# A two-layer trunk on one core: the last feed-forward output, with both column halves of a token tile in a row

## The chip, the cores and the metric

The kernel runs on one core of a Trainium2 chip. The metric is the device time of one execution in microseconds (us), as the median of several runs. The engines of the core are TensorE (PE; its weight loads are shown as PEld), VectorE (DVE), ScalarE (ACT) and GpSimd (POOL); SyncE (SP) issues most DMA transfers.

## What is computed

One inference step of a trunk of two layers, for 512 latent tokens and 128 prompt tokens of width 1024, in float32. Each layer does this (`ctx` are cached keys, values and states, which the latent tokens read; the mixers are differential attention, a gated delta network and HGRN2):

```python
def trunk_layer(x, mod, w_in, w_out, ..., ln_g, ln_b, w_ffn_in, w_ffn_out, ctx):
    shift_m, scale_m, gate_m, shift_f, scale_f, gate_f = jnp.split(mod, 6, axis=-1)
    z = (x * (1 + scale_m) + shift_m) @ w_in
    o, k_c, v_c, s_d, s_h = token_mixers(z, ..., ctx)
    x = layer_norm(ALPHA * x + gate_m * (o @ w_out), ln_g[0], ln_b[0])
    gt, up = jnp.split((x * (1 + scale_f) + shift_f) @ w_ffn_in, 2, axis=-1)
    x = layer_norm(ALPHA * x + gate_f * ((jax.nn.silu(gt) * up) @ w_ffn_out), ln_g[1], ln_b[1])
    return x, k_c, v_c, s_d, s_h
```

The feed-forward's hidden width is 2816. The outputs are x of both token groups, and keys, values and states of the prompt.

## The kernel before

**Tiling.** The 640 tokens are five tiles of 128 (tau 0 to 3 latent, 4 prompt; `NT` is 5). Products run in split float32: each operand is a high part and a low rest, and a product is three passes over them. A weight block is loaded by SP into `raw` (L256), cast to its high part `hl` by ScalarE (L275), and VectorE forms the rest; that is `unit`. `mm` (L175) is every matmul and `tt` (L178) every two-operand elementwise operation, whichever engine it is given, so these two lines hold much of the trace.

**Stages of a layer.** The input projections (names pa, pb, pc), the mixers (attention with the scores `pas`, HGRN with the products `ph` and its transposes `pth`; the modulation vectors of what follows, `psm`, run among them), the output projection `pop` with residual and normalisation, whose transposes are `pta`, and the feed-forward. In the mixers HGRN's queries `hq` (L588) and values `hv` (L589) and the attention's operands `aqs`, `aks`, `ack`, `avf` (L1154 to L1187) come from device memory, all by SP's queue.

**The feed-forward's output.** Its 22 blocks of 128 hidden columns go in six parts (`FF_PARTS`); the last holds four blocks, 18 to 21. A part's product is added into the residual `r` of each token tile, in two column halves of 512 (`nh`), so there are ten groups (nh, tau) of 12 matmuls each for the last part. Each group goes into a bank of PSUM `pfo`; VectorE multiplies it by the gate (`ft`, two buffers), GpSimd adds it to `r` (VectorE for tile 4), and VectorE takes the half's statistics (L1724). When half 1 of a tile is done, the tile can be normalised. In layer 0 that is `ln_next`: statistics joined, GpSimd takes the power -0.5, then for tiles 0 to 2 ScalarE normalises, VectorE scales and GpSimd shifts; for tiles 3 and 4 two VectorE operations do it (L545, L546). The result `xmf` is transposed by TensorE (`ptf`, L503) and split into `xT` by ScalarE (L505) and VectorE; from there layer 1's projections start, first `pbg`. In layer 1 it is `ln_last`: for tiles 0 to 2 the halves are shared between ScalarE with GpSimd and VectorE, for tiles 3 and 4 VectorE does all (L576, L577), and SP writes the output.

**What sets the order.** The order of the groups is the list `order` (L1700). A group is issued no sooner than the end of the group four before it (`OPEN`). The instructions of the whole kernel are then put in order for each engine by a scheduler that plays them on a timeline of its own; the code's order is its input, and its choices run on through what follows.

Of the kernel before, what the change touches and what calls it, by code (L numbers as in the profile page):

```python
# [25 lines left out]
NT = NTOK // P  # L26
# [85 lines left out]
def tile_trunk(  # L112
# [30 lines left out]
    def psum_phase(**classes):  # L143

        PS.clear()
        for names, tags in classes.items():
            cyc = {"tags": tags, "i": 0}
            for n in names.split("_"):
                PS[n] = cyc
# [15 lines left out]
    def psS(cls, name):  # L165
        ps = ps_next(cls, [P, 512], name)
        return ps[:, 0, :] if len(ps.shape) == 3 else ps
# [9 lines left out]
    def tt(eng, out, a, b, op):  # L177
        return eng.tensor_tensor(out, a, b, op)  # L178
# [22 lines left out]
    def pool(name, side):  # L201
        cm_ = tc.tile_pool(name=name, bufs=1, side=side, reuse_waits="tile")
        return cm_, cm_.__enter__()

    def close(cm_):
        cm_.__exit__(None, None, None)
# [90 lines left out]
    def gemm_N(ps, n, aT, tau, units, first=True, last=True):  # L297

        tot = sum(len(ks) for _, ks in units)
        j = 0  # L300
        for u, ks in units:
            for i, k in enumerate(ks):
                for q, (wi, xi) in enumerate(PASSES):
                    end = mm(ps[:, :n], (aT(xi, k) if callable(aT) else aT[:, xi, k])[:, tau * P:(tau + 1) * P], u[:, wi, i, :],
                       start=(first and j == 0 and q == 0), stop=(last and j == tot - 1 and q == 2))
                j += 1
        return end
# [4 lines left out]
    def rowunit(w, k0, nk, c0, n):  # L312
        return unit(w[k0 * P:(k0 + nk) * P, c0:c0 + n].rearrange("(k p) n -> p k n", p=P), nk, n)

    def bg_units(l):
        return [(rowunit(w_in[l], k0, nk, C_BG, NB), list(range(k0, k0 + nk))) for k0, nk in ((0, 3), (3, 3), (6, 2))]
# [171 lines left out]
    def rowload(pool, src, tag, t=None):  # L488
        if t is None:
            t = pool.tile([P, D], F32, tag=tag, bufs=1, name=tag)  # L490
        S.dma_start(t, src.partition_broadcast(P))
        return t

    def modvec(l, i, j):
        return modrow[l][j, i * D:(i + 1) * D]
# [13 lines left out]
    def affine(l, si, mi, ln, pool, tag, bufs):  # L509


        raw = pool.tile([P, 1024], F32, tag=tag, bufs=bufs, name="aff")
        v = raw[:32, :256].rearrange("p (k n) -> p k n", k=4)
        rows = [modrow[l][:, i * D:(i + 1) * D].rearrange("j (q n) -> j q n", n=64) for i in (si, mi)]
        for j in range(2):
            for k, src in enumerate((rows[0][j], rows[1][j], ln_g[ln], ln_b[ln])):
                S.dma_start(v[16 * j:16 * j + 16, k], src if k < 2 else src.rearrange("(q n) -> q n", n=64))
        V.tensor_scalar_add(v[:, 0], v[:, 0], 1.0)
        tt(V, v[:, 3], v[:, 0], v[:, 3], ALU.mult)
        tt(V, v[:, 1], v[:, 1], v[:, 3], ALU.add)  # L520
        tt(V, v[:, 0], v[:, 0], v[:, 2], ALU.mult)
        for j in range(2):
            for k in range(2):
                S.dma_start(rows[k][j], v[16 * j:16 * j + 16, k])

    def affine_rows(pool, l, si, mi, pre=None):

        return [[rowload(pool, modvec(l, i, j), f"{nm}{j}", pre and pre[2 * j + k])
                 for k, (i, nm) in enumerate(((si, "sc"), (mi, "sh")))] for j in range(2)]
# [20 lines left out]
    def ln_tile(r, mv, rs, g, b, tau):  # L550
        V.scalar_tensor_tensor(r[tau], r[tau], mv[:, tau, 0:1], g, ALU.subtract, ALU.mult)  # L551
        V.scalar_tensor_tensor(r[tau], r[tau], rs[:, tau, 0:1], b, ALU.mult, ALU.add)
# [795 lines left out]
    for l in range(DEPTH):  # L1348
# [258 lines left out]
        def pair_a(f):  # L1607
            if f not in gts:
                gate_unit(f)
            gt_ = gts.pop(f)  # L1610
            a_ = psS("g", f"pfa{l}_{f}")
            prod(a_, gt_, 0, "11")
            if 2 <= f < AHEAD:
                s1, sg = xtra[:, (f - 2) * 960:(f - 2) * 960 + HT], xtra[:, (f - 2) * 960 + HT:(f - 1) * 960]
            else:
                s1 = fp.tile([P, HT], F32, tag="s1", bufs=2, name=f"s1_{l}_{f}")
                sg = fp.tile([P, NTOK], F32, tag="sg", bufs=2, name=f"sg{l}_{f}")
            A.copy(s1, a_[:, :HT])
            prod(a_, gt_, 4, "12", start=False)
            A.activation(sg[:, :HT], a_[:, :HT], AF.Silu)  # L1620
            part_a[f] = (s1, sg)
# [46 lines left out]
        for part, (f0, f1) in enumerate(FF_PARTS):  # L1668
            nk = f1 - f0
            last = part == len(FF_PARTS) - 1  # L1670
            for f in range(f0, f1):
                end = pair_b(f, f - f0)
                if AHEAD - 1 <= f < NFF - 1:
                    pair_a(f + 1)
                if part == 0:
                    with tc.issue_after(end.ins):
                        for tau in range(f, NT if f == f1 - 1 else f + 1):
                            ln_tile(r, mv, rs, lg, lb_, tau)
            if part == 0 and l + 1 < DEPTH:
                affine(l + 1, 1, 0, (l, 1), praw, "raw", 3)  # L1680
            if part == 0:
                gf = [rowload(None, modvec(l, 5, j), None, t_) for j, t_ in enumerate((lg, lb_))]
            if last:
                close(sc_)
                close(hx)
                lc, lp = pool(f"M{l}", "left")
                WB[0] = 3
                if l + 1 < DEPTH:
                    rows = affine_rows(lp, l + 1, 1, 0)
                else:  # L1690
                    HL["seq"], HL["i"] = [(phl, "hl", 4), (lp, "hl", 2)], 0
                    lg2, lb2 = (rowload(lp, x_[l, 1], n_) for x_, n_ in ((ln_g, "lg2"), (ln_b, "lb2")))
                    psum_phase(g_n=PP1 + PP2 + QQ + RR)

            def out_units(nh):
                return [(rowunit(Wo, f0 + k0, 2, nh * 512, 512), [k0, k0 + 1]) for k0 in range(0, nk, 2)]

            usn, ends = {}, []
            skew = 1 if last else NT
            order = [(nh, tau) for i in range(NT + skew) for nh, tau in ((0, i), (1, i - skew)) if 0 <= tau < NT]  # L1700
            if last and l + 1 < DEPTH:
                HL["seq"], HL["i"] = [(phl, "hl", 4)], 0
                usn[0] = out_units(0)
                HL["seq"], HL["i"] = [(fp, "hb", 1), (lp, "hl", 1)], 0
                usn[1] = out_units(1)
                HL["seq"], HL["i"] = [(phl, "hl", 4)], 0
                bgu = bg_units(l + 1)
            for nh, tau in order:
                us = usn[nh] if nh in usn else usn.setdefault(nh, out_units(nh))
                cs = slice(nh * 512, (nh + 1) * 512)  # L1710
                j = 0 if tau < LT else 1
                ps = psS("n", f"pfo{l}_{part}_{nh}_{tau}")
                with ExitStack() as es:
                    if last and len(ends) >= OPEN:
                        es.enter_context(tc.issue_after(ends[-OPEN].ins))
                    ends.append(gemm_N(ps, 512, h_, tau, us))
                tmp = fp.tile([P, 512], F32, tag="ft", bufs=2, name="ft")
                tt(V, tmp, ps, gf[j][:, cs], ALU.mult)
                if part == 0:
                    V.scalar_tensor_tensor(r[tau][:, cs], r[tau][:, cs], ALPHA, tmp, ALU.mult, ALU.add)  # L1720
                else:
                    tt(V if last and tau >= 4 else G, r[tau][:, cs], r[tau][:, cs], tmp, ALU.add)
                if last:
                    V.bn_stats(st[tau][:, nh, :], r[tau][:, cs])  # L1724
                    if nh == 1 and l + 1 < DEPTH:
                        ln_next(lp, r[tau], st[tau], mv, rs, rows[j], xT, tau, f"f{l}_{tau}")
                    elif nh == 1:
                        dst = y_sample[0, tau * P:(tau + 1) * P, :] if tau < LT else y_prompt[0]
                        ln_last(r[tau], st[tau], mv, rs, lg2, lb2, tau, dst)
# [47 lines left out]
```

## Time and profile before

| | |
|---|---|
| Median of 3 runs | 2084.02 us (2083.7 to 2092.38) |
| Profiled execution | 2080.84 us |
| Span of its trace | 2078.9 us |
| PE / DVE / POOL / ACT busy | 92% / 69% / 42% / 38% of the span |
| Mean granted TensorE clock | 0.956 of full |
| Layer 0's mixers (first pas to first pop) | 351.45 to 521.88 us |
| Layer 0's last feed-forward output and what follows it | 1027.77 to 1071 us |
| Layer 1's mixers | 1370.19 to 1542.56 us |
| Layer 1's output projection | 1542.56 to 1620.68 us |
| Last feed-forward output, to the last normalisation | 2039.49 to 2075.30 us |

The span is the time from the trace's first instruction to its last. A share of busy time is a mean over stages that have different limits, so each stage has to be read by itself. In a row of the timeline, the bracket is the time that the engine stood idle before it, with an arrow to what released it.

### The profile page before, as it was taken

What the parts mean: (1) busy time and instruction counts of PE and PEld (TensorE: products, weight loads), DVE (VectorE), ACT (ScalarE), POOL (GpSimd) and SP (SyncE); (2) the same over time, 40 slices, a digit from 0 to 9 for tenths busy, and PEclk for the clock granted to TensorE, in tenths of its full rate; (3) what the DMA queues carried; (4) which work ended last, traced back from release to release, by engine and by line L of the source; (5) the groups of instructions that cost most, each with busy time, mean ns of one, the idle gap of its engine ahead of it and who ended that gap; (6) DMA issues with size and microseconds to landing.
All of it is one profiled execution on the core that took longest, in us unless ns stands there. A gap on an engine that the chain in (4) does not pass through costs nothing. (4 is left out here: it accounts for less than half of the span.)

```text
span 2078.9 us, 37821 instructions
## 1 busy us (share of the span) xinstructions
PE 1905.8 (92%) x14914; PEld 1676.6 (81%) x14914; DVE 1444.5 (69%) x2515; ACT 791.4 (38%) x1563; POOL 880.2 (42%) x986
## 2 busy tenths in 40 slices
PE   7999997788978999999999989977899799999996
PEld 5988986566758899989989979765687779989895
DVE  5458525898488866667676783459867897667677
ACT  3542322566143334333336323236752434334331
POOL 0375235775142132435155924358642311532444
PEclk7999999899999999999999999989899899999998
DMA  8423215866353323222434341376434233223222
GB/s 284 131 79 121 93 57 140 217 200 205 137 179 90 115 82 92 72 82 73 142 96 130 108 131 57 102 169 214 143 148 147 83 110 91 72 82 93 80 72 81
DMA packets 243255, 249.36 MB, mean 120 GB/s; under 512 B 19354, under 2 KB 190342, under 8 KB 243078
## 3 DMA queue, kind: packets, MB, share of 16 engines
q1 hardware_dynamic: 240486, 245.11, 38.6%
q8 instruction: 118, 1.93, 0.4%
q10 hardware_dynamic: 2592, 1.84, 0.3%
q14 instruction: 59, 0.48, 0.1%
HBM read 218.72 MB, written 28.18 MB: 119 GB/s over the span
## 5 line engine op out<-in xcount | busy, mean ns | idle before, releaser
L178 DVE TENSOR_TENSOR hl<-raw,hl 128x1024 fp32r<-128x1024 f32 (+1 forms) x210 | 281.4, 1344 | 87.5 <-ACT hl L275 70.6
L175 PE MATMUL pfo<-hl,ha 128*128 128x512 f32 x1320 | 312.7, 395 | 1.6 <-ACT hl L275 1.1
L175 PEld LDWEIGHTS pfo<-hl,ha 128*128 128x128 f32 x1320 | 246.2, 187 | 60.5 <-DVE ha L178 1.4
L178 POOL TENSOR_TENSOR r<-r,ft 128x512 f32<-128x512 f32 x96 | 143.4, 1513 | 241.1 <-DVE ft L178 238.4
L178 POOL TENSOR_TENSOR t<-raw 128x512 f32<-128x512 f32 x44 | 66.2, 1504 | 337.0 <-DMA raw<-in_w_ffn_in_dram 168.2
L175 PE MATMUL pfc<-sx,hl 128*128 128x320 f32 x1056 | 173.8, 313 | 9.5 <-ACT hl L1553 7.2
L175 PE MATMUL pfa<-xT,hl 128*128 128x320 f32 x1056 | 173.2, 314 | 4.5 <-DVE hl L178 3.0
L275 ACT CAST hl<-raw 128x1024 fp32r<-128x1024 f32 (+2 forms) x122 | 125.8, 1036 | 132.9 <-DMA raw<-in_w_ffn_out_dram 49.7
L175 PEld LDWEIGHTS pfc<-sx,hl 128*128 128x128 f32 x1056 | 161.8, 190 | 12.9 <-ACT hl L1553 7.8
L1553 ACT CAST hl<-raw 128x1024 fp32r<-128x1024 f32 x88 | 92.0, 1051 | 203.8 <-PE pfo L175 105.4
L175 PEld LDWEIGHTS pfa<-xT,hl 128*128 128x128 f32 x1056 | 161.9, 192 | 7.3 <-DVE hl L178 3.8
L175 PE MATMUL paq<-xT,hl 128*128 128x320 f32 x768 | 123.9, 318 | 0.6 <-ACT az L1241 0.6
L175 PE MATMUL pop<-hl,xT 128*128 128x512 f32 x480 | 120.7, 403 | 0.0
L175 PEld LDWEIGHTS paq<-xT,hl 128*128 128x128 f32 x768 | 116.3, 191 | 3.5 <-issue 1.2
L175 PEld LDWEIGHTS pop<-hl,xT 128*128 128x128 f32 x480 | 88.4, 190 | 24.8 <-issue 6.6
L178 DVE TENSOR_TENSOR ft<-pfo,lg 128x512 f32<-128x512 f32 x96 | 63.9, 683 | 51.2 <-PE pfo L175 41.5
L178 DVE TENSOR_TENSOR t<-raw,t 128x512 f32<-128x512 f32 x88 | 73.9, 840 | 36.0 <-POOL t L178 35.8
L178 POOL TENSOR_TENSOR hK<-hK,hT 64x256 f32<-64x256 f32 x120 | 87.0, 725 | 27.1 <-PE ph L175 21.2
L175 PE MATMUL pfd<-xT,h 128*128 128x320 f32 x528 | 86.2, 313 | 9.6 <-DVE u L178 9.6
L175 PE MATMUL pbq<-xT,hl 128*128 128x320 f32 x576 | 89.5, 312 | 1.2 <-DVE hl L178 0.4
L175 PE MATMUL pfb<-sx,hl 128*128 128x320 f32 x528 | 89.2, 311 | 0.6 <-DVE hl L178 0.6
L175 PEld LDWEIGHTS pfd<-xT,h 128*128 128x128 f32 x528 | 80.0, 190 | 11.1 <-issue 8.5
(409 smaller groups left out, 4198.6 us busy)
## 6 DMA issues: line engine op xcount, KB each, us to landing
raw<-in_w_ffn_in_dram SPq DMA_DIRECT2D x96, 512.0 KB
raw<-in_w_mod_dram SPq DMA_DIRECT2D x80, 512.0 KB
raw<-in_w_in_dram SPq DMA_DIRECT2D x56, 512.0 KB
raw<-in_w_ffn_out_dram SPq DMA_DIRECT2D x44, 512.0 KB
pc<-in_w_mod_dram SPq DMA_DIRECT2D x8, 1024.0 KB
raw<-in_w_out_dram SPq DMA_DIRECT2D x16, 512.0 KB
qksc<-az SPq DMA_DIRECT2D x16, 320.0 KB
qkhi<-azs SPq DMA_DIRECT2D x16, 256.0 KB
```

Of the source, the lines that this page charges most:

```text
L175: return nc.tensor.matmul(out, lhsT, rhs, start=start, stop=stop, **kw)
L178: return eng.tensor_tensor(out, a, b, op)
L275: A.copy(hl[:, 0, :kt * n], raw[:, :kt * n])
L1553: A.copy(tile_[:, 0, :n], raw)
```

## The change

The list of groups is made with a skew between the halves. With a skew of 1, half 0 runs one tile ahead of half 1 in the last part: (0,0), (0,1), (1,0), (0,2), (1,1), (0,3), (1,2), (0,4), (1,3), (1,4), written (nh, tau). With a skew of 0 it is tile by tile: (0,0), (1,0), (0,1), (1,1) and so on to (0,4), (1,4). The other parts keep all tiles of half 0 before half 1. Both layers run this line. No instruction is added or taken away.

```diff
             usn, ends = {}, []
-            skew = 1 if last else NT
+            skew = 0 if last else NT
             order = [(nh, tau) for i in range(NT + skew) for nh, tau in ((0, i), (1, i - skew)) if 0 <= tau < NT]
             if last and l + 1 < DEPTH:
```

The orders of the engines move in several places. The first is TensorE at the end of layer 0's feed-forward. The names are `pfo_part_nh_tau`; `ptf_tau_column` are the transposes of the normalised tile, `pbg` is layer 1's first projection. Before:

```order
L175 MATMUL pfo_5_1_2_10596<-hl,ha_6699 128x512 x12
L175 MATMUL pfo_5_0_4_10636<-hl,ha_6699 128x512 x12
L175 MATMUL pfo_5_1_3_10653<-hl,ha_6699 128x512 x12
L175 MATMUL pfo_5_1_4_10690<-hl,ha_6699 128x512 x12
L503 MATMUL ptf_0_0_10508<-c_ident,xmf_0_10502 128x128 x4
L503 MATMUL ptf_0_4_10515<-c_ident,xmf_0_10502 128x128 x4
L175 MATMUL pbg_0_10740<-hl,xT_4128 128x272
L503 MATMUL ptf_1_0_10565<-c_ident,xmf_1_10559 128x128 x4
L175 MATMUL pbg_0_10740<-hl,xT_4128 128x272 x12
```

The same place now:

```order
L175 MATMUL pfo_5_0_3_10619<-hl,ha_6699 128x512 x12
L175 MATMUL pfo_5_1_3_10636<-hl,ha_6699 128x512 x12
L175 MATMUL pfo_5_0_4_10673<-hl,ha_6699 128x512 x12
L175 MATMUL pfo_5_1_4_10690<-hl,ha_6699 128x512 x12
L503 MATMUL ptf_0_0_10491<-c_ident,xmf_0_10485 128x128 x4
L503 MATMUL ptf_0_4_10498<-c_ident,xmf_0_10485 128x128 x4
L175 MATMUL pbg_0_10740<-hl,xT_4128 128x272
L503 MATMUL ptf_1_0_10548<-c_ident,xmf_1_10542 128x128 x4
L175 MATMUL pbg_0_10740<-hl,xT_4128 128x272 x12
```

Half 1 of tile 3 has changed places with half 0 of tile 4; the rows behind the last pfo are as they were.

The second place is SP's queue in layer 1's mixers, where HGRN's loads hq and hv stand among the attention's loads for head 2. Before:

```order
L697 DMA hS_3_14575<-in_state_hgrn_dram 64x4x64
L588 DMA hq_14578<-cqs_436 64x4x640 x2
L589 DMA hv_14579<-cis_440 128x5x256
L1162 DMA ack_2_14523<-in_cache_attn_k_dram 128x128
L1164 DMA ack_2_14523<-in_cache_attn_k_dram 128x64 x2
L1154 DMA aqs<-qkhi_444 64x512
```

Now, after one hq load and the same loads L1154 to L1159 of head 2:

```order
L1160 DMA aks<-qksc_442 128x128
L1164 DMA ack_2_14523<-in_cache_attn_k_dram 128x64
L256 DMA raw<-in_w_mod_dram 128x1024
L588 DMA hq_14578<-cqs_436 64x4x640
L589 DMA hv_14579<-cis_440 128x5x256
L1429 DMA xT_14419<-osc_430 128x5x256
```

The second hq load and hv have gone from ahead of head 2's loads to behind them. On TensorE HGRN's first products then stand behind more of the attention's, and its last transposes behind 19 matmuls of the output projection (pop_0_0 and the first of pop_0_1).

The third place is TensorE in layer 1's output projection, where `pop_nh_tau` are its groups, `psm` modulation vectors and `pta` the transposes of a finished tile. Before:

```order
L175 MATMUL pop_1_1_16641<-hl,xT_14419 128x512 x9
L175 MATMUL pop_1_2_16693<-hl,xT_14419 128x512 x16
L175 MATMUL psm_5_16536<-raw,cm 32x256 x4
L175 MATMUL pop_1_2_16693<-hl,xT_14419 128x512 x2
L175 MATMUL psm_5_16536<-raw,cm 32x256 x4
L175 MATMUL pop_1_2_16693<-hl,xT_14419 128x512 x6
L175 MATMUL pop_1_3_16747<-hl,xT_14419 128x512 x6
L1495 MATMUL pta_0_0_16599<-c_ident,xma_0_16593 128x128 x4
```

The same place now:

```order
L175 MATMUL pop_1_1_16641<-hl,xT_14419 128x512
L175 MATMUL pop_1_2_16693<-hl,xT_14419 128x512 x4
L175 MATMUL pop_1_3_16747<-hl,xT_14419 128x512 x8
L175 MATMUL pop_1_4_16810<-hl,xT_14419 128x512 x10
L175 MATMUL psm_5_16536<-raw,cm 32x256 x4
L175 MATMUL pop_1_4_16810<-hl,xT_14419 128x512 x3
L175 MATMUL psm_5_16536<-raw,cm 32x256 x4
L175 MATMUL pop_1_4_16810<-hl,xT_14419 128x512 x11
L175 MATMUL psm_5_16536<-raw,cm 32x256 x12
```

The half 1 groups of tiles 0 to 3 are now finished close together, and the transposes pta come only after the last pop.

## Rows read from the trace of the kernel before

**Rows 1.** The page's first part: busy us of each engine, share of span, instructions.

```profile
PE 1905.8 (92%) x14914; PEld 1676.6 (81%) x14914; DVE 1444.5 (69%) x2515; ACT 791.4 (38%) x1563; POOL 880.2 (42%) x986
```

**Rows 2.** Busy time by stage; columns in the first line, one stage a row.

```profile
core 0: us, PE busy (x) PEld busy (x) DVE busy (x) ACT busy (x) POOL busy (x), PEclk, DMA share, GB/s
521.88:604.14 82.26, 76.59 (x424) 54.79 (x427) 48.70 (x74) 18.15 (x30) 18.24 (x17) 0.96 0.48 160
1031.47:1066.89 35.42, 31.50 (x163) 27.26 (x162) 32.83 (x52) 9.18 (x12) 25.83 (x26) 0.90 0.49 150
...
1075.47:1370.19 294.72, 281.31 (x2917) 256.03 (x2916) 175.83 (x347) 101.95 (x185) 148.28 (x167) 0.98 0.33 104
1370.19:1542.56 172.37, 136.53 (x1408) 109.34 (x1407) 143.42 (x308) 107.08 (x318) 115.73 (x192) 0.87 0.55 157
...
1542.56:1620.68 78.12, 69.32 (x362) 52.35 (x360) 51.23 (x79) 17.82 (x27) 19.03 (x18) 0.95 0.51 175
2044.12:2075.30 31.18, 18.39 (x79) 14.43 (x77) 28.30 (x45) 2.45 (x3) 23.80 (x19) 0.87 0.17 68
```

**Rows 3.** Timeline of PE, end of layer 0: start, us, operation, count, [idle before <-releaser].

```profile
1027.77 22.51 PE L175 MATMUL pfo<-hl,ha 128*128 128x512 f32 x96
...
1055.46 1.11 PE L503 MATMUL ptf<-c_ident,xmf 128*128 128x128 f32 x4 [3.68 <-DVE rs L538]
1056.23 3.07 PE L175 MATMUL pbg<-hl,xT 128*128 128x272 f32 x12
...
1062.09 2.88 PE L175 MATMUL pbg<-hl,xT 128*128 128x272 f32 x21
...
1069.99 1.04 PE L503 MATMUL ptf<-c_ident,xmf 128*128 128x128 f32 x8
```

**Rows 4.** Timeline of DVE, the same stretch: tile 4's last normalising operation.

```profile
1065.62 1.27 DVE L546 SCALAR_TENSOR_TENSOR xmf<-xmf,rs,sh 128x1024 f32<-128x1024 f32 x1
```

**Rows 5.** One microsecond of the same stretch, columns as in rows 2.

```profile
1058.00:1059.00 1.00, 1.00 (x6) 1.00 (x6) 1.00 (x1) 0.00 (x0) 0.95 (x1) 0.50 0.90 309
```

**Rows 6.** Timeline of SP's queue in layer 1's mixers.

```profile
1387.56 1.27 SPq L588 DMA_DIRECT2D hq<-cqs  x2
...
1391.85 0.47 SPq L1154 DMA_DIRECT2D aqs<-qkhi  x1
...
1405.97 0.43 SPq L1160 DMA_DIRECT2D aks<-qksc  x1
```

**Rows 7.** Timeline of PE: HGRN's first products and last transposes, layers 0 and 1.

```profile
379.92 1.15 PE L175 MATMUL ph<-hq,hK 128*64 128x64 f32 x32 [1.43 <-DMA hq<-cqs]
...
515.42 0.44 PE L503 MATMUL pth<-c_ident,ho 128*128 128x128 f32 x2 [1.78 <-POOL ho L178]
...
1397.03 1.00 PE L175 MATMUL ph<-hq,hK 128*64 128x64 f32 x26 [2.28 <-DMA hq<-cqs]
...
1542.26 0.44 PE L503 MATMUL pth<-c_ident,ho 128*128 128x128 f32 x2 [0.26 <-POOL ho L178]
```

**Rows 8.** Waits of SP's queue, 1384 to 1407: us in total, times, longest.

```profile
SPq L1158 <- DMA hv<-cis: 3.5, 1, 3.5
SPq L1156 <- DMA hq<-cqs: 2.6, 1, 2.6
SPq L1155 <- DMA hq<-cqs: 1.5, 1, 1.5
```

**Rows 9.** Timeline of DVE and of PE, layer 1's output projection.

```profile
1578.63 0.69 DVE L178 TENSOR_TENSOR rt<-pop,gm 128x512 f32<-128x512 f32 x1 [4.14 <-PE pop L175]
...
1618.74 1.94 PE L1495 MATMUL pta<-c_ident,xma 128*128 128x128 f32 x8 [7.74 <-DVE xma L546]
```

**Rows 10.** Timeline of PE and of DVE at the kernel's end.

```profile
2039.49 23.02 PE L175 MATMUL pfo<-hl,ha 128*128 128x512 f32 x98
...
2070.04 2.27 DVE L577 SCALAR_TENSOR_TENSOR r<-r,rs,lb 128x1024 f32<-128x1024 f32 x1 [0.33 <-POOL rs L178]
...
2074.01 1.29 DVE L577 SCALAR_TENSOR_TENSOR r<-r,rs,lb 128x1024 f32<-128x1024 f32 x1 [0.44 <-POOL rs L178]
```

## The prediction

> **What bounds the kernel now.** I read the table of busy time first [rows 1]: TensorE is busy in 1905.8 of 2078.9 us (92%), VectorE in 69%. A mean of 92% would say that only TensorE's own work counts, and the edit adds and takes away no instruction. So the stages come next, one row each [rows 2]. In the projections after the first layer (1075.47 to 1370.19) TensorE works 281.31 of 294.72 us: what reaches this stretch earlier ends it earlier. In three stages TensorE waits and VectorE is nearest to full: the end of layer 0, from the first gate product to tile 4's last normalisation (32.83 of 35.42 us), the mixers of layer 1 (143.42 of 172.37), and the kernel's tail (28.30 of 31.18). The edited loop is the work of the first and the last of these. The code's order is input to a scheduler, and by the orders shown it also moves loads in layer 1's mixers and the tiles of layer 1's output projection. Those are four places; elsewhere I count the edit at nothing, since the orders differ there by little and the same work stands in each stage.
>
> All terms are changes of the time, negative where it gets shorter.
>
> **Part 1, the end of layer 0.** The TensorE rows [rows 3] show where it waits: it finishes the feed-forward's output (begun at 1027.77), transposes tile 0, does one matmul, then stands 3.68 us for tile 1's normalisation (the releaser is its rs), and then alternates between transposes and the next layer's first projection. With the edit the second half of each of the tiles 0 to 3 comes one group of 12 matmuls earlier, and tile 4's is last in both orders. A group is 12 x 22.51/96 = 2.81 us [rows 3], so the 3.68 us wait shrinks to 0.9 at best. What is late next? The last transposes, of tile 4, start at 1069.99 [rows 3], and VectorE ends the normalisation that they read at 1065.62 + 1.27 = 1066.89 [rows 4]. Over the 35.42 us up to there VectorE is idle 35.42 - 32.83 = 2.59 us [rows 2]. Two bounds follow: with VectorE's end where it is, tile 4's transposes can come earlier by at most 1069.99 - 1066.89 = 3.10; if all VectorE idle goes too, by 3.10 + 2.59 = 5.69. The other bound is 0: the wait is only cut into smaller ones, before each tile. Stepping the new order with the durations shown, TensorE's one wait becomes several short ones for VectorE's xT subtractions, and tile 4's transposes come at about 1068. I take **-2.0, from -5.7 to 0**; the busy projections behind (281.31 of 294.72) pass it on.
>
> After the 3.68 us wait TensorE's clock is low: 0.50 granted, the 1.2 GHz level [rows 5]. There 12 matmuls of the projection take 3.07 us, and later 21 take 2.88 [rows 3], 0.256 and 0.137 each, so the low level costs 12 x 0.119 = 1.4 us once. That is no further term: the upper bound of -5.7 holds for any clock, because VectorE sets it.
>
> The Trainium skill (TensorE: Matmul & The Clock Gate, Part 1) says the clock has two levels and follows how busy TensorE has been; shorter waits would then keep it at 2.4 GHz, and the sum would be 1.4 us lower, by this row. That the clock is at half right behind the one long wait agrees with it.
>
> **Part 2, layer 1's mixers.** Before, the queue of SP issues both hq loads at 1387.56 and hv behind them, then head 2's attention loads from 1391.85 to 1405.97 + 0.43 [rows 6]. In the new order the second hq load and hv stand behind all of these, and behind a weight load. HGRN's first matmuls wait for exactly that hq: 1.43 us in layer 0, 2.28 in layer 1 [rows 7]. The loads now ahead fill 1406.40 - 1391.85 = 14.55 us; of this 3.5 + 2.6 + 1.5 = 7.6 is the queue waiting for hq and hv themselves [rows 8], which may go or may become waits for other transfers. So HGRN starts 7.0 to 14.6 us later. Against this stand two things. HGRN needs less time when it competes less: from its first ph to its last transpose layer 0 takes 515.42 - 379.92 = 135.5 us and layer 1 takes 1542.26 - 1397.03 = 145.2 [rows 7], a spread of 9.7 with the same work. And the output projection starts before HGRN's last transposes now: 19 of its matmuls stand ahead, at 69.32/362 = 0.19 us each [rows 2] 3.6 us. That bounds the term: 7.0 - 9.7 - 3.6 = -6.3 and +14.6 with neither. Attention is further ahead when HGRN begins, and VectorE has 143.42 us of work in the stage's 172.37 [rows 2], in whichever order the two ask. Work that is done earlier isn't left over at the end, so I take **0, from -6.3 to +14.6**.
>
> **Part 3, layer 1's output projection.** Before, VectorE's first residual product waits 4.14 us for TensorE, and at the end TensorE waits 7.74 us for VectorE's tile 4 before the last transposes [rows 9]. In the new order half 1 of tiles 0 to 3 is finished close together, and all pta transposes and 16 more modulation matmuls stand behind the last pop. The time between the last pop and the last transposes is then filled, at best the whole 7.74 us wait; but five normalisations bunch on VectorE, which has 51.23 of 78.12 us to do [rows 2]. The nearest price for a worse order of this stage is layer 0's, 82.26 us for the same work, 4.1 more. Stepping both orders from the last half-0 tile, VectorE ends tile 4 some 2 us earlier, with more of its casts left for after. I take half of that: **-1, from -2 to +4**.
>
> **Part 4, the tail.** TensorE begins the last part's output at 2039.49; VectorE starts the first ft at 2044.12 and ends the last scaling at 2074.01 + 1.29 = 2075.30 [rows 2, 10]. It is idle for 31.18 - 28.30 = 2.88 us of this [rows 2]. The edit completes tiles 0 to 3 earlier by a step each, tile 4 not at all: its half 1 is still last. What it can take is VectorE's idle time. Two of the idle pieces are waits for POOL's rs right before the last two L577 [rows 10], which depend on tile 4's and on tile 3's own chain and stay: 0.33 + 0.44. That leaves 2.11. L577 shows a second price: 2.27 and 1.29 us for the same shape [rows 10], the longer one beside POOL's work on the same tiles; with more tiles ready at once the longer one may come up oftener. I take **-1, from -2.1 to 0**.
>
> The Trainium skill (SBUF — State Buffer, "SBUF: two separate sides") gives VectorE and GpSimd one shared port pair, held by one at a time; by it each step that starts earlier on VectorE pays in waits on POOL, and the tail gains nothing (the sum would be -3). The 2.27 beside 1.29 agrees.
>
> **Sum.** -2.0 + 0 - 1 - 1 = -4.0. The profiled execution is 2078.9 of span + 1.94 = 2080.84, which gives 2076.84; it is 3.18 under the median of 2084.02, and on the median the sum gives 2084.0 - 4.0 = **2080.0**. About 0.5% (10.4 us: 2073.6 to 2094.4) is what a measurement of this kernel can tell from no change.
>
> **The rivals.**
> *Slower: HGRN starts too late.* The mechanism is the moved hq load. For it: the wait of the first ph for this very load, in both layers [rows 7], and HGRN's transposes as the last mixer work before the projection. Against: VectorE's load, which does not grow. It decides once the delay is more than what HGRN gets shorter by plus 3.6. At the full +14.6, with parts 1, 3 and 4 giving half of their sum (-2): 2084.0 + 12.6 = **2096.6**.
> *Faster: the mixers improve as well.* HGRN runs in layer 0's 135.5 us and starts only 7 later, so part 2 gives -6.3; part 1 reaches its -5.7; parts 3 and 4 as above: -6.3 - 5.7 - 2 = -14.0, **2070.0**. For it: attention further ahead, so fewer turns for HGRN to wait for. Against: VectorE is 83% busy there, with the same work in either order.
> *It only moves the waits.* VectorE is nearly full in both edited loops (93% and 91%), its work is the same, and the last tile comes when it came: 0, **2084.0**. For it: the releasers in [rows 9, 10] are VectorE and POOL, not the tile order. Against: the 3.68 us wait, for one tile's normalisation alone.
>
> **Chances.** Forecast 0.42, only moved 0.20, faster 0.22, slower 0.16. The forecast's own range, with part 2 within 6 either way, is 2071 to 2088. For 8 in 10 the range takes in the faster rival and stops short of the slower one: 2066 to 2096. By the bound of 0.5%: faster 0.22, same 0.42 + 0.20 = 0.62, slower 0.16. Both the slower and the faster case come from part 2, the widest bound.
>
> **What would show it.** Part 1: the single wait of 3.68 us before tile 1's transposes is gone or under 2, tile 4's transposes start about 2 us sooner counted from the first pfo of the last part, VectorE at over 93% between. Part 2: the first ph of layer 1 comes 7 to 15 us later counted from the stage's start, the stage from first pas to first pop within 6 us of 172.4. Part 3: the wait before the last pta is under 7.7, the stage at 76 to 80 us. Part 4: first ft to the last L577 at 29 to 31 us. Wrong would be: a new long TensorE wait anywhere between 1075 and 2044, where I count nothing, or HGRN's end past attention's by more than 5 us.

## The result, and the profile after

The changed kernel is slower: 2096.3 us (median of 7 runs, 2093.68 to 2099.64) against 2086.61 us for the kernel before (median of 7 runs); the ratio is 1.0058, with an interval of 1.0043 to 1.0072. By the ratio that is about 12 us of loss, by the two medians 9.7, where 4 us of gain was forecast. The profiled execution has a span of 2095.0 us, 16.1 more than that of before.

Only a part of that is busy time. The first part of the page of after, to be held against [rows 1]:

```profile
PE 1916.4 (91%) x14914; PEld 1682.1 (80%) x14914; DVE 1448.3 (69%) x2515; ACT 791.4 (38%) x1563; POOL 879.5 (42%) x986
```

VectorE has 3.8 us more and TensorE 10.6, for the same instructions. The stages say where the time went. To set stages of two traces beside each other I use marks that both have: the last matmul `pci` of layer 1's projections (the mixers run from there to the first `pop`), the first `pop`, and the first `pfc` matmul of layer 1's feed-forward (the output projection with everything that VectorE owes behind it). The busy time by stage of the kernel before, cut at these marks and at the first half 1 product of VectorE (`rt`), with columns as in [rows 2]:

```profile
1340.55:1542.56 202.01, 161.39 (x1795) 132.00 (x1794) 159.09 (x352) 112.30 (x333) 131.54 (x212) 0.89 0.54 155
...
1542.56:1578.63 36.07, 36.07 (x166) 29.54 (x168) 17.57 (x29) 5.50 (x10) 2.86 (x5) 1.00 0.68 248
1578.63:1640.59 61.96, 48.57 (x285) 37.61 (x284) 51.66 (x70) 24.42 (x37) 23.35 (x17) 0.89 0.34 102
```

The same three stretches of the changed kernel, and its tail from the first `ft` to the last L577:

```profile
1338.35:1546.46 208.11, 165.02 (x1790) 131.90 (x1789) 158.43 (x351) 110.96 (x325) 128.68 (x209) 0.86 0.53 147
...
1546.46:1593.93 47.47, 47.47 (x220) 38.63 (x219) 17.05 (x29) 6.79 (x16) 3.52 (x8) 1.00 0.56 201
1593.93:1654.59 60.66, 42.59 (x233) 32.84 (x231) 52.46 (x70) 24.14 (x37) 27.32 (x17) 0.77 0.35 105
...
2059.83:2091.41 31.58, 18.16 (x78) 14.24 (x76) 29.56 (x45) 2.45 (x3) 24.19 (x19) 0.82 0.17 67
```

The mixers take 208.11 us where they took 202.01, with the same work for VectorE (158.43 and 159.09). The output projection takes 47.47 + 60.66 = 108.13 where it took 36.07 + 61.96 = 98.03, and all of the loss lies ahead of VectorE's first half 1 product. Up to there VectorE has the same 17 us of work in both kernels; behind it come 52 us of work in 61 to 62 us in both. Only the moment at which that work can begin has moved, from 36.07 to 47.47 us after the first `pop`, by 11.40.

The row of VectorE at that moment, which answers to the first of [rows 9], and the row of TensorE ahead of it, in the changed kernel:

```profile
1562.47 30.19 PE L175 MATMUL pop<-hl,xT 128*128 128x512 f32 x132
...
1593.93 0.69 DVE L178 TENSOR_TENSOR rt<-pop,gm 128x512 f32<-128x512 f32 x1 [13.73 <-PE pop L175]
```

TensorE is busy with `pop` all that time, but with the first three weight units of four tiles; the fourth unit, which would complete tile 0, comes behind them. VectorE waits 13.73 us, where it waited 4.14. The other side of the stage is that the last `pop` ends sooner after the first, 58.9 us where it was 64.2, and then TensorE waits for VectorE. The stretch from the last `pop` to the first `pfc`, first in the kernel before and then in the changed one:

```profile
1606.71:1640.59 33.88, 20.49 (x114) 18.96 (x113) 31.73 (x36) 16.13 (x26) 12.66 (x7) 0.80 0.21 61
...
1605.37:1654.59 49.22, 31.15 (x169) 25.40 (x169) 41.77 (x45) 20.55 (x34) 23.39 (x14) 0.71 0.30 92
```

When TensorE ends its last `pop`, VectorE has 41.77 us of the stage's work left, where it had 31.73. The 10.0 us more are about what the stage got longer by.

In the mixers the second hq load went where the order said. SP's queue in the changed kernel, which answers to [rows 6], and TensorE's first HGRN products, which answer to the third of [rows 7]:

```profile
1386.10 0.58 SPq L588 DMA_DIRECT2D hq<-cqs  x1
...
1388.13 0.47 SPq L1154 DMA_DIRECT2D aqs<-qkhi  x1
...
1396.98 0.43 SPq L1160 DMA_DIRECT2D aks<-qksc  x1
...
1398.40 0.60 SPq L588 DMA_DIRECT2D hq<-cqs  x1
...
1406.04 2.19 PE L175 MATMUL ph<-hq,hK 128*64 128x64 f32 x36 [2.15 <-DMA hq<-cqs]
```

HGRN starts 1406.04 - 1338.35 = 67.7 us after the last `pci`, where it started 1397.03 - 1340.55 = 56.5 after it: 11.2 us later. By the mark that the prediction used, the first `pas`, the mixers begin at 1364.44 in the changed kernel and at 1370.19 in the kernel before [rows 2]; that is 3.5 us sooner after the last `pci` (26.1 instead of 29.6). Counted from there HGRN starts 14.8 us later, and the stage takes 182.02 us instead of 172.37:

```profile
1364.44:1546.46 182.02, 140.14 (x1401) 109.32 (x1402) 145.63 (x318) 106.86 (x314) 115.32 (x192) 0.84 0.53 146
```

At the end of layer 0 nothing moved. TensorE there, to be held against [rows 3]; the row of 96 `pfo` is the last part's output without its first two groups, which stand further ahead in both kernels:

```profile
1030.08 22.50 PE L175 MATMUL pfo<-hl,ha 128*128 128x512 f32 x96
...
1058.09 1.09 PE L503 MATMUL ptf<-c_ident,xmf 128*128 128x128 f32 x4 [4.00 <-DVE mv L533]
...
1072.40 1.03 PE L503 MATMUL ptf<-c_ident,xmf 128*128 128x128 f32 x8
```

From the start of this row of `pfo` to tile 4's transposes it is 42.32 us; it was 42.22. The single wait before tile 1 is 4.00 us, where 3.68 stood.

### The profile page after: what moved, and what is told of

Read it like the earlier page. It is cut to its first block, busy times and chain, and to the rows that moved or that the text cites. A ratio compares the mean times of both kernels' runs of the same rounds, so it can differ in the third digit from the quotient of the medians.

```text
span 2095.0 us, 37826 instructions
## 1 busy us (share of the span) xinstructions
PE 1916.4 (91%) x14914; PEld 1682.1 (80%) x14914; DVE 1448.3 (69%) x2515; ACT 791.4 (38%) x1563; POOL 879.5 (42%) x986
## 4 chain that ended last, share of the span: by engine, by line
PE 53%; DVE 16%; POOL 8%; DMA 8%; issue 5%; ACT 3%; SPq 1%; POOLq 0%; ACTq 0%; DVEq 0%
PE pfo L175 12%; PE pfd L175 6%; PE pfa L175 6%; PE pfc L175 6%; PE pop L175 5%; PE pfb L175 3%; PE pci L175 2%; DMA raw<-in_w_mod_dram 2%; PE pcf L175 2%; DVE hq L178 2%; DVE hl L178 2%; POOL r L178 1%; PE psm L175 1%; DMA osc<-doh 1%; PE pav L175 1%
## 5 line engine op out<-in xcount | busy, mean ns | idle before, releaser
L175 PEld LDWEIGHTS pfc<-sx,hl 128*128 128x128 f32 x1056 | 161.8, 191 | 16.7 <-ACT hl L1553 11.4
```

Source lines behind the costliest of these rows:

```text
L175: return nc.tensor.matmul(out, lhsT, rhs, start=start, stop=stop, **kw)
```

## The experiments

Three theories stood against each other. **A**: the loss is in layer 1's output projection, where VectorE gets its half 1 tiles late. **B**, later called **H**: it is in layer 1's mixers, by the late hq load. **C**: the edited loops themselves lose time. The table has all runs, with the stages between the marks above read from one trace each. "Mixers" is last `pci` to first `pop`, "from pas" is first `pas` to first `pop`, "output" is first `pop` to first `pfc`, "tail" is from the long row of `pfo` that ends layer 1's last part (2039.49 in the kernel before, [rows 10]) to the end of the span. A single stage differs by some microseconds between traces of the same order: the four kernels at the head, whose mixers stand in one order, have 202.0 to 206.9.

| kernel | ratio to before, interval | mixers | from pas | output | tail |
|---|---|---|---|---|---|
| before | 1 | 202.0 | 172.4 | 98.0 | 39.41 |
| l1_only | 0.9997 (0.9985 to 1.0010) | 204.2 | 172.6 | 98.0 | 40.05 |
| l0_two_swaps | 1.0008 (0.9995 to 1.0022) | 206.9 | 174.6 | 99.7 | 39.40 |
| before_seq_out | 0.9990 (0.9975 to 1.0004) | 203.0 | 171.7 | 96.7 | 39.40 |
| the changed kernel | 1.0058 (1.0043 to 1.0072) | 208.1 | 182.0 | 108.1 | 40.04 |
| l0_only | 1.0052 (1.0035 to 1.0069) | 208.6 | 183.0 | 106.9 | 39.41 |
| after_seq_out | 1.0018 (1.0003 to 1.0034) | 209.6 | 182.6 | 99.3 | 40.03 |
| after_seq_out_2 | 1.0025 (1.0012 to 1.0038) | 209.7 | 182.8 | 99.3 | 40.04 |
| after_hq_only | 1.0009 (0.9994 to 1.0024) | 198.3 | 172.1 | 108.5 | 40.04 |
| after_hq_first | 0.9974 (0.9962 to 0.9985) | 198.3 | 171.7 | 100.3 | 40.05 |
| before_late_hq | 1.0036 (1.0019 to 1.0053) | 212.0 | 181.2 | 99.2 | 39.40 |
| after_early_hq | 1.0051 (1.0031 to 1.0071) | 215.1 | 188.7 | 99.8 | 40.23 |
| before_hq_first | 0.9998 (0.9981 to 1.0016) | 203.2 | 172.1 | 100.2 | 39.41 |
| l0_three_swaps | 1.0062 (1.0043 to 1.0081) | 208.9 | 181.3 | 100.6 | 39.41 |

### The edit in one layer at a time

The edit in layer 1 alone, against the kernel before:

```diff
-            skew = 1 if last else NT
+            skew = 1 - (l == 1) if last else NT
```

> The edit in layer 1 alone, that is in the kernel's tail; every order before the last feed-forward part is that of the kernel before. Theory A (the changed kernel loses in layer 1's output projection, where VectorE gets the half 1 tiles late) and theory B (it loses in layer 1's mixers, where the hq load is late) both expect the time of before within 2 us. Theory C (the edited loops themselves lose) expects 3 to 6 us more than before.

The ratio is 0.9997: the edit in the tail is worth nothing that the timing can tell. In the trace the tail is 40.05 us instead of 39.41, and so it is, within 0.2, in all kernels of the table that carry the edit in layer 1; the others have 39.40 or 39.41. So it costs 0.6 us. C falls for the tail. The edit in layer 0 alone, against the kernel before:

```diff
-            skew = 1 if last else NT
+            skew = 1 - (l == 0) if last else NT
```

> The edit in layer 0 alone; layer 1's mixers and output projection stand in the changed kernel's order, the tail in that of before. A and B: the whole loss of the changed kernel, 9 to 11 us over before. C: about half of it, 4 to 6.

The ratio is 1.0052, the whole loss within the intervals, as A and B had it. It comes through layer 0's exchange of groups; in the mixers and the output projection the engines' orders are those of the changed kernel.

### The end of layer 0 by itself

Two of the four exchanges, against the kernel before:

```diff
+            if last and l == 0:
+                order = [(0, 0), (1, 0), (0, 1), (1, 1), (0, 2), (0, 3), (1, 2), (0, 4), (1, 3), (1, 4)]
```

> Of the edit's four exchanges in layer 0's last part the first two alone (tiles 0 and 1 with both halves in a row); the orders of layer 1's mixers, output projection and tail are those of before on each engine. Theory A: within 2 us of before, and tile 4's transposes at the end of layer 0 start as long after the first pfo as before, within 1 us. Theory C, that the order at the end of layer 0 itself costs: 3 us or more over before.

The ratio is 1.0008, inside the 2 us. From the long row of `pfo` to tile 4's transposes its trace has 42.77 us, where before has 42.22 and the changed kernel 42.32. C falls here too, for half of the exchanges; for all of them the row at 1072.40 above shows no change, and l0_only has 42.59. Three of the four exchanges, against the kernel before:

```diff
+            if last and l == 0:
+                order = [(0, 0), (0, 1), (1, 0), (1, 1), (0, 2), (1, 2), (0, 3), (1, 3), (0, 4), (1, 4)]
```

> In layer 0's last part three of the edit's four exchanges (halves tile by tile from tile 1 on, tile 0's second half stays third); by the orders, layer 1's mixers and output projection then stand exactly as before, and so does layer 1's tail. A and B: within 2 us of before. C: 3 to 5 us over before.

This run did not test what its expectation says. The premise on the orders was wrong: in its trace HGRN starts 73.8 us after the last `pci` (56.5 in before), so its mixers do not stand as before. It lost as much as the changed kernel, 1.0062, with mixers of 208.9 us and an output projection of 100.6; both hq loads stand behind head 2's loads here. But it loses at the end of layer 0 as well. TensorE's wait before tile 1 in its trace:

```profile
1057.28 1.09 PE L503 MATMUL ptf<-c_ident,xmf 128*128 128x128 f32 x4 [6.10 <-DVE xT L178]
```

Tile 4's transposes start 1072.02 - 1026.17 = 45.85 us after the long row of `pfo`, 3.6 later than in before. So an order of these groups can cost what C said, and this one does; the edit's own order does not (42.32 and 42.59).

### The output projection, tile after tile

In layer 1 a tile's half 1 is queued behind the end of the tile before it; the changed kernel's mixers stay as they are. Against the changed kernel:

```diff
-            gemm_N(ps, 512, xT, tau, us1)
+            with ExitStack() as es:
+                if l == 1 and len(pops) >= 1:
+                    es.enter_context(tc.issue_after(pops[-1].ins))
+                pops.append(gemm_N(ps, 512, xT, tau, us1))
```

> The changed kernel, and in layer 1's output projection half 1 of a tile is issued no sooner than the end of the tile before it, so that the tiles finish one after the other as before; layer 1's mixers keep the changed kernel's order. A: 7 to 11 us less than the changed kernel, 0 to 3 over before; VectorE's wait before the first half 1 product falls from 13.7 us to about 4. B: no more than 3 us less than the changed kernel, 7 or more over before.

> The changed kernel with half 1 of the output projection tile after tile, hq late, once more beside the kernel that has hq first. H: 3 to 5 us over before and over that kernel; R: the same time as that kernel within 1.5 us.

The ratio falls from 1.0058 to 1.0018 and, in the second measurement, 1.0025: 7 to 8 us come back. VectorE's first half 1 product in after_seq_out:

```profile
1582.48 0.69 DVE L178 TENSOR_TENSOR rt<-pop,gm 128x512 f32<-128x512 f32 x1 [1.29 <-PE pop L175]
```

It starts 1582.48 - 1547.45 = 35.0 us after the first `pop`, as in before (36.07), and the whole stage is 99.3 us instead of 108.1. That is what A expected, with a wait of 1.29 us where about 4 was expected. What is left over before, 0.2%, has the mixers of 209.6 us beside it, and in the traces the mixers' order is the changed kernel's on every engine.

> The kernel before, and in layer 1's output projection half 1 of a tile is issued no sooner than the end of the tile before it; the mixers stand as before. A control for the run of the changed kernel with the same constraint. Theory A (that run regained the time because its output projection got its order back) expects the time of before within 2 us; the rival, that the constraint is a gain for any order, expects 4 us or more less than before.

The control has the same constraint with the order of before: 0.9990, an interval that holds 1. The constraint is no gain in itself, and what after_seq_out won is the order that it got back.

### The late hq load

> The kernel before with half 1 of the output projection tile after tile, and in layer 1's mixers the second hq load and hv are issued only behind head 2's attention loads, at the place that they have in the changed kernel. Theory H (the late hq load is what costs the changed kernel some 4 us in the mixers) expects 3 to 6 us over the same kernel without the late load. The rival R (the load is hidden, and the mixers' other moves cost the time) expects 0 to 1.

```diff
-            S.dma_start(q5[ds_], cqs[l].rearrange("(h j) t -> j h t", j=64))
-        S.dma_start(v5, cis[l].rearrange("(t p) c -> p t c", p=P))
+            with ExitStack() as es:
+                if l and d:
+                    es.enter_context(tc.issue_after(KPD[max(KPD)].ins))
+                S.dma_start(q5[ds_], cqs[l].rearrange("(h j) t -> j h t", j=64))
+                if d:
+                    S.dma_start(v5, cis[l].rearrange("(t p) c -> p t c", p=P))
...
-        S.dma_start(kp, qksc[l][1, h, :, NLAT:])
+        KPD[l, h] = S.dma_start(kp, qksc[l][1, h, :, NLAT:])
```

The diff is against before_seq_out. `KPD` holds for each head the attention's load of the prompt's keys, L1160 in [rows 6]. The constraint on the output projection is in this kernel too. The late load costs 2090.27 - 2081.26 = 9.0 us against before_seq_out of the same measurement, more than H expected; the mixers go from 203.0 to 212.0, the output projection from 96.7 to 99.2. Their order is not that of before any more, nor that of the changed kernel.

> The changed kernel with half 1 of the output projection tile after tile, and layer 1's second hq load and hv issued by GpSimd's queue, so that they do not stand behind the attention's loads. H: 3 to 5 us less than the same kernel with the late load, within 1.5 us of before. R: the same time as with the late load, 3 to 5 us over before.

```diff
-            S.dma_start(q5[ds_], cqs[l].rearrange("(h j) t -> j h t", j=64))
-        S.dma_start(v5, cis[l].rearrange("(t p) c -> p t c", p=P))
+            (G if l and d else S).dma_start(q5[ds_], cqs[l].rearrange("(h j) t -> j h t", j=64))
+        (G if l else S).dma_start(v5, cis[l].rearrange("(t p) c -> p t c", p=P))
```

The diff is against after_seq_out. This run went against H: 1.0051, 5 to 7 us more than with the late load. HGRN did start sooner (62.5 us after the last `pci`, where after_seq_out has 69.6), and still the mixers took 215.1 us, the longest of all. Its longest wait of TensorE is another one, 6.1 us for the attention's load `ack`, where the changed kernel has 1.7. The run changes two things, the queue and the order that the scheduler makes around it, and does not tell them apart. So the next run moved the load within SP's queue, again from after_seq_out:

```diff
-            S.dma_start(q5[ds_], cqs[l].rearrange("(h j) t -> j h t", j=64))
-        S.dma_start(v5, cis[l].rearrange("(t p) c -> p t c", p=P))
+            with (tc.high_priority() if l else ExitStack()):
+                S.dma_start(q5[ds_], cqs[l].rearrange("(h j) t -> j h t", j=64))
+                if d:
+                    S.dma_start(v5, cis[l].rearrange("(t p) c -> p t c", p=P))
```

> The changed kernel with half 1 of layer 1's output projection tile after tile, and both hq loads and hv of layer 1 given priority, so that they stand in SP's queue ahead of head 2's attention loads as in the kernel before (no other queue is used). Theory H (what the mixers lose is the late hq load): within 2 us of before, HGRN's first products 47 to 50 us after the mark in the projections from which the mixers are counted, the mixers 193 to 197 us. The rival R (the late load is not it): 3 to 5 us over before, mixers at 199 or more.

The ratio is 0.9974 (0.9962 to 0.9985): 11.7 us under after_seq_out_2, its neighbour in the same measurement (2076.34 and 2088.01; H had expected 3 to 5), and faster than both kernels of this study. H expected to be level with before; the mixers are shorter than before's instead, with VectorE's work within 3.3 us of theirs. They are still longer than the 193 to 197 us that H expected, and HGRN starts 57.5 us after the last `pci`, not 47 to 50. The busy time of after_hq_first in the mixers:

```profile
1339.96:1538.24 198.28, 159.58 (x1790) 129.01 (x1789) 155.78 (x353) 111.54 (x326) 131.39 (x210) 0.90 0.54 155
```

> The same priority for hq and hv, without the constraint on the output projection, whose half 1 tiles are finished close together as in the changed kernel. If the output projection's order is a loss of its own: 8 to 11 us over the kernel with the constraint, VectorE's wait before the first half 1 product 10 us or more. If it is only a consequence of the mixers' late end: within 3 us of the kernel with the constraint.

With the load first and the output projection left as the change has it, the ratio is 1.0009, 2083.82 - 2076.34 = 7.5 us over after_hq_first, a little under the 8 to 11 expected. VectorE's first half 1 product waits as long as in the changed kernel, although the mixers end early:

```profile
1581.45 0.69 DVE L178 TENSOR_TENSOR rt<-pop,gm 128x512 f32<-128x512 f32 x1 [13.73 <-PE pop L175]
```

So the output projection's order is a loss by itself and no consequence of the mixers, whose order is the same in these two kernels. With the two conditions set one by one, the four kernels add up: the output projection's order is worth 0.33 to 0.40% with the late load (1.0058 to 1.0025 or 1.0018) and 0.35% with the early one (1.0009 to 0.9974); the load is worth 0.49% (1.0058 to 1.0009) and 0.44 to 0.51%. (1.0058 and 1.0018 come from other measurements than the rest.) Together that is more than the change lost, and the rest is the 0.26% by which after_hq_first is faster than before.

> The fastest version so far (hq and hv of layer 1 with priority, half 1 of the output projection tile after tile) without the edit, that is with half 0 one tile ahead in both layers. If the gain of that version over before comes from the two additions: the same ratio to before within 0.15%, about 0.997. If the edit takes part in it: the time of the kernel before with the output projection constraint alone, ratio 0.999 or more.

The diff is that of after_hq_first, with the skew left at 1. The ratio is 0.9998, and the mixers take 203.2 us: the edit takes part in the gain. In the order of before the early load brings nothing, since it was early there already.

The column "from pas" parts the two effects. It has 171.7 to 174.6 us in the seven kernels whose hq and hv loads stand ahead of head 2's loads, and 181.2 to 183.0 in the six with a late load; either group holds three different orders of the mixers. after_early_hq, with 188.7, is in neither. What the edit gains lies, in the traces, ahead of the first `pas`: attention starts 25.6 to 27.6 us after the last `pci` in the kernels whose layer 0 has the edit or three of its exchanges, and 29.6 to 32.2 in all others. Why it starts sooner stays open.

## Why the prediction was wrong

**Part 1, the end of layer 0: forecast -2.0, measured +0.1.** It ends at a bound that was given, 0. The step that failed is that the wait of 3.68 us shrinks because a group of matmuls comes sooner. The wait is for VectorE, which works 32.83 of 35.42 us there [rows 2]; with the new order its work comes in another order and ends no sooner (tile 4's L546 ends 39.5 us after the row of `pfo` starts, 39.1 before), and the wait is still one wait, of 4.00 us. The cost of the low clock behind it was paid as before: the next 12 matmuls of the projection take 3.07 us in both kernels. The rival that the edit only moves the waits described this part.

**Part 2, the mixers: forecast 0, from -6.3 to +14.6; measured about +5.** The three kernels with the late load and no other tampering in the mixers, and the repeat of one, have 208.1 to 209.7 us, mean 209.0; the four with the order of before have 202.0 to 206.9, mean 204.0. By the prediction's own marks, first `pas` to first `pop`, it is +9.7, and a gain of 3.5 stands ahead of the first `pas`, where it counted nothing. The delay of HGRN's start was forecast at 7.0 to 14.6 and came out at 14.8 from the first `pas`, 11.2 from the last `pci`. What I set against it was partly misread. I took 1542.26 [rows 7] for HGRN's last transposes; the trace of before has two more:

```profile
1549.40 0.39 PE L503 MATMUL pth<-c_ident,ho 128*128 128x128 f32 x2
```

So HGRN took 1549.40 - 1397.03 = 152.4 us there, and the output projection had started 6.8 us ahead of its end already. The last transpose of the changed kernel:

```profile
1551.12 0.27 PE L503 MATMUL pth<-c_ident,ho 128*128 128x128 f32 x1
```

HGRN takes 145.1 us now, 7.3 less, so that part of the counterweight was real. The 3.6 us for the output projection's start were not: its lead on HGRN's last transpose shrank to 4.7 us, by 2.2. Together that is 14.8 - 7.3 + 2.2 = 9.7. "Work that is done earlier isn't left over at the end" was the step that failed: VectorE's work is the same, but its idle time between the last `pci` and the first `pop` grew from 42.9 to 49.7 us.

That the late load is the cause is shown in two ways, by putting it into the kernel before (+9.0 us) and by taking it out of the changed one (-11.7). Every move of this load makes the scheduler place the mixers anew, so no pair of runs changes the load alone; that three orders with it in time and three with it late fall into two groups, some 10 us apart from the first `pas`, speaks for the load and against the orders. One early load, by GpSimd's queue, made the mixers longer, and that stays open.

**Part 3, the output projection: forecast -1, from -2 to +4; measured about +10.** This is the term that was mis-sized most, and by more than its range. To the last `pta`, where the prediction ended the stage, the traces have 83.2 us against 78.1, so +5.1; the rest is work that VectorE still owes behind it, up to the first `pfc`. 108.1, 106.9 and 108.5 us with the bunched order stand against 96.7 to 100.6 for all others. I priced the end of the stage, where TensorE waits for VectorE [rows 9], and stepped the order from the last half 0 tile with an eye on when VectorE ends tile 4. That wait did go, from 7.74 us to 2.14 before the last `pta`, and the stage got longer all the same. The row that mattered was the other one of [rows 9], the 4.14 us that VectorE waits for its first half 1 tile. Behind that moment VectorE has 52 us of work in some 61 us, so most of what the first tile comes later is lost to the stage, whatever the last tile does: 11.4 us later cost 10.1 here, and from after_seq_out to the changed kernel 12.4 us later cost 8.8. The order's rows showed it: half 1 of tile 0 was completed only behind the first three units of tiles 1 to 3. Layer 0's 82.26 us, which I took as the nearest worse price, has tiles that finish one by one and is no bound for this.

**Part 4, the tail: forecast -1, from -2.1 to 0; measured +0.6.** VectorE's idle time did shrink, from 2.88 to 31.58 - 29.56 = 2.02 us, but its busy time grew by 1.26 with the same 45 instructions. One shape shows it, L577 on half a tile; first in the kernel before, then the longest in the changed kernel with GpSimd's row at that moment:

```profile
2054.10 0.74 DVE L577 SCALAR_TENSOR_TENSOR r<-r,rs,lb 128x512 f32<-128x512 f32 x1
...
2074.61 1.86 DVE L577 SCALAR_TENSOR_TENSOR r<-r,rs,lb 128x512 f32<-128x512 f32 x1
...
2074.62 1.30 POOL L178 TENSOR_TENSOR r<-r,ft 128x512 f32<-128x512 f32 x1
```

The other five of this shape in the two tails, three before and two now with at most 0.1 us of GpSimd's work beside them, take 0.74 or 0.75 us.

The prediction named this second price, without a number. The Trainium skill (SBUF — State Buffer, "SBUF: two separate sides") gives VectorE and GpSimd one shared port pair, held by one at a time; the longer row agrees with it, though no run here took GpSimd's work away to show it.

**The sum.** The traces give 0.1 + 5 + 10 + 0.6 = 15.7 us for the four places, against 12 us timed (9 to 15 by the interval). The rest lies within what single traces of one order differ by: elsewhere the changed kernel's trace has 2.3 us more ahead of the edit, 4.6 less in layer 1's projections and 1.5 more in its feed-forward. The projections differ by as much between traces of the same order. The slower rival named the right sign and the mechanism of the smaller half, the late hq load. It had 0.16 of the chances; its time, 2096.6, is near the measured one by a coincidence, since it gave the mixers all of the loss and the output projection none. "Elsewhere nothing" held in the main: between the last `pfo` of layer 0 and the mixers, and inside layer 1's feed-forward, no new wait over 2 us appeared. TensorE's wait before the first `pfc`, at the end of the output projection, grew from 3.26 to 6.93 us.

## What to carry to other kernels

Where a scheduler makes the order, the price of a small edit lies where the orders come apart later, and that may be far from the edited loop. In a stage in which one engine has a fixed amount of work left, look for the moment at which it gets the first piece, not at when the other engine ends its last: a producer that brings four tiles along together is as busy as before and still starves the consumer. And before a stage of a single trace is taken at its word, put traces of the same order beside it; here one stage differed by 5 us with nothing changed in it.

## What was not expected of the hardware

VectorE's half-tile scaling (L577, 128x512) took 0.74 us in one place and 1.86 in another, with a GpSimd operation on `r` beside it in the second. And the granted TensorE clock was lower where TensorE waited more: 0.89 in the output projection's second stretch before and 0.77 after. There 285 matmuls had taken 48.57 us of busy time, and 233 took 42.59, not all of the same shapes; the stretch as a whole was 1.3 us shorter.
